# The last group of modulation columns, moved from the second down projection to the first

## The chip, the cores and the metric

The kernel runs on one core of one Trainium2 chip. The metric is device time in microseconds (us) of one execution, as the median of several runs. The engines are named as in the profile: PE (TensorE matmul) and PEld (its weight loads), DVE (VectorE), ACT (ScalarE), POOL (GpSimd) and SP (SyncE, whose queue issues all the loads and stores spoken of here). L12 is line 12 of the kernel before.

## What is computed

One layer of a streaming encoder on 512 tokens of 1024 channels, in float32: a SwiGLU feed-forward block, a token mixer (a gated delta rule beside latent attention) and a second feed-forward block. Each is scaled and shifted by columns that depend on the condition `c` alone:

```
mod = silu(c) @ w_ada + b_ada                                  # 9 x 1024 columns
sh1, s1, g1, sh2, s2, g2, sh3, s3, g3 = split(mod, 9)
h = rms(x) * (1 + s1) + sh1
x = x + 0.5 * g1 * ((silu(h @ w_gate) * (h @ w_up)) @ w_out)   # 1024 -> 2 x 2816 -> 1024
h = rms(x) * (1 + s2) + sh2
x = x + g2 * mixer(h)
h = rms(x) * (1 + s3) + sh3
x = x + 0.5 * g3 * ((silu(h @ w_gate2) * (h @ w_up2)) @ w_out2)
```

The change concerns the last 1024 of these columns, `g3`, which only the residual add of the second feed-forward block reads.

## The kernel before

**Layout and precision.** Channels lie on the 128 partitions, tokens along the free axis, so `x` is eight tiles of 128x512 (`self.xT`). A float32 product is made of three matmuls (`mm3`, L475 to L477): each operand is split into a high part and the rest, and high x high, high x low and low x high are summed in PSUM. A weight unit is 128 output columns by up to eight rows of 128: it is loaded to a raw tile `wr`, ACT casts the high part `wh` (L234) and DVE subtracts the low part `wl` (L235). Raw, high and low tiles have four buffers each.

**First down projection** (`down`, first call). Eight output tiles t = 0 to 7, each with three weight units of 8, 8 and 6 row blocks (`KPARTS`), so three parts of 24, 24 and 18 matmuls. After each part `down` gives side work a turn (`side.step`). A finished tile is added to `xT` by DVE (L1026), ACT squares it and DVE adds the square to `accum` for the next norm (L736 to L741). Tile 7 is made in two halves of 256 tokens in an order written out by hand (`in_order`), with the norm's sums over partitions (L761) and the first modulated tiles of the mixer between. The same function also makes the mixer's constants from tile 5 on: its first step (L1329 to L1341) issues small loads (to `cw`, `vb` and the positions), the second transposes `cw` on PE (L1345), the third transposes the positions (L1352).

**Modulation columns.** Group 0 (g1, sh2) is made in the first feed-forward block, groups 1 (s2, g2), 2 (sh3, s3) and 3 (g3) as side work by `ada_rest`. A group has four chunks of 512 columns, group 3 has two. For a chunk, eight row blocks of `w_ada` are loaded as 128x512 tiles (`ar`, SP) and summed on DVE with the entries of silu(c) as scalars (L826 for the first, L828 for the rest, into `aa`). One side step takes two row blocks: two loads and two sums. `ada_columns` then sums over partitions by a matmul with ones (L885), copies the rows (ACT, L888), transposes them back to columns (PE, L892), adds the bias (DVE, L896) and, for some columns, adds 1 or halves them (L901, L903). The loop of `ada_rest` runs these columns between the next group's sums; after the last group it adds two empty steps and then the columns.

**Second down projection** (`last_down`). `PLAN` lists its pieces: tiles 0 and 1 over all 22 row blocks ("all"), the tail (last six row blocks) of tiles 4 to 7, and then pairs of tiles by a form of seven products in place of eight (`seven_down`, L1244), for which `act_sums` makes sums of activations on DVE (L1127). Group 3 is made beside tile 1 and ended before the first tail (`side.flush`). Until then the accumulators of tiles 0, 1 and the first tail wait in `held`; the adds to `xT` (L1161), which need g3, follow together. A tile of the output is transposed on PE (L1294), copied by ACT and stored by SP (`store`); tiles 0 and 1 are stored inside the first pair by seven products.

**Order.** At the build, a scheduler makes one fixed queue per engine. It follows the order of the program among the instructions that are ready by its own estimate, so a weight split can come long before its place in the program, and PE work that is not ready goes behind later matmuls. Buffers are handed out in the same pass: 56 slots of 128x512 (`slots`) hold activations, `ar`, `aa` and most temporaries. At run time each engine works through its queue in order.

Of the kernel before, what the change touches and what calls it, by code (L numbers as in the profile page):

```python
# [99 lines left out]
class Block:  # L100
# [918 lines left out]
    def down(self, act, gate, norm=None):  # L1019

        nc = self.nc
        accum = self.slot(s="na") if norm else None
        full, ha, hb = slice(0, NT), slice(0, HALF), slice(HALF, NT)

        def update(t, ts, p):
            nc.vector.scalar_tensor_tensor(out=self.xT[t][:, ts], in0=p[:, ts], scalar=self.mod[gate][:, t:t + 1],  # L1026
                                           in1=self.xT[t][:, ts], op0=ALU.mult, op1=ALU.add)

        def finish(t, ts, p):
            update(t, ts, p)  # L1030
            if norm:
                self.square_in(t, ts, accum)

        def parts(t, ts, units=None, by=8, late=False):
            p = self.acc()
            for i, (k0, n) in enumerate(KPARTS):
                u = units[i] if units else self.next_unit()
                for k in range(0, n, by):
                    self.dense(p, u, act, ts, k, min(k + by, n), FT - 1, k0)
                    yield  # L1040
            if late:
                held.append((t, ts, p))
            elif norm and ts != full:
                update(t, ts, p)
            else:
                finish(t, ts, p)

        last = KT - 1
        side, held = Side(), []
        side.add(self.ada_rest((1, 2) if norm else (3,)))  # L1050
        if norm:
            self.consts = Side()
            self.consts.add(self.mixer_consts())

        def split_first():
            p = self.acc()
            for i, (k0, n) in enumerate(KPARTS):
                u = self.next_unit()
                for k in range(0, n, 2):
                    while any(not isinstance(a, tuple) for a in act[:k0 + k + 5]):  # L1060
                        self.splits.step()
                    self.dense(p, u, act, full, k, min(k + 2, n), FT - 1, k0)
                yield
            if norm:
                finish(0, full, p)
            else:
                held.append((0, full, p))

        for t in range(last):
            if norm and t == 1:  # L1070
                self.masks()
            for i, _ in enumerate(parts(t, full, late=not norm and t < 2) if t else split_first()):
                if t:
                    side.step(4 if not norm else 2)
                if norm and t == 5:
                    self.consts.step()
                if not norm and t > 2:
                    if i == 1:
                        self.store(t - 2, range(NB))
                elif not norm and t == 2:  # L1080
                    if i == 0:
                        side.flush()
                        for h in held:
                            finish(*h)
                    elif i == 1:
                        self.store(0, range(NB))
        units = [self.next_unit(ahead=0) for _ in KPARTS]
        if not norm:
            for i, _ in enumerate(parts(last, ha, units)):
                if i < 2:  # L1090
                    self.store(last - 2 + i, range(NB))
            for i, _ in enumerate(parts(last, hb, units)):
                if i == 1:
                    self.store(last, range(2))
            self.store(last, range(2, 4))
            return None
        with self.in_order():
            self.preload(3)
            for i, _ in enumerate(parts(last, ha, units)):
                if i == 0:  # L1100
                    side.step()
                if i == 1:
                    self.prefetch(1)
            side.flush()
            sa = self.square_half(last, ha)
            self.new_h()
            pa, pb = self.aux(), self.aux()
            na, nb = self.norm_half(0, pa, norm), self.norm_half(1, pb, norm)
            for i, _ in enumerate(parts(last, hb, units, 2)):
                if i == 0:  # L1110
                    self.add_sums(pa, accum[:, ha], first=True)
                    self.add_sums(pb, accum[:, hb], first=True)
                if i == 2:
                    self.add_sums(pa, sa, last=True)
                if i == 2 or i > 4:
                    next(na)
                if i == 4:
                    self.prefetch(2)
            self.prefetch(3)
            sb = self.square_half(last, hb)  # L1120
        return na, nb, lambda: self.add_sums(pb, sb, last=True)
# [30 lines left out]
    def last_down(self, act, gate):  # L1152

        nc = self.nc
        full = slice(0, NT)
        side, sums, parts7, ended, held = Side(), Side(), Side(), [], []
        side.add(self.ada_rest((3,)))
        sums.add(self.act_sums(self.whole))

        def update(t, ts, src):  # L1160
            nc.vector.scalar_tensor_tensor(out=self.xT[t][:, ts], in0=src, scalar=self.mod[gate][:, t:t + 1],  # L1161
                                           in1=self.xT[t][:, ts], op0=ALU.mult, op1=ALU.add)

        def ahead():
            self.preload(1)
            parts7.add(self.raws.pop(0)())

        def stores():
            while ended:
                self.store(ended.pop(0), range(NB))  # L1170
                yield

        for at, (kind, t) in enumerate(PLAN):
            after = [k for k, _ in PLAN[at + 1:at + 3]] + ["all"] * 2
            if kind in SEVENS:
                w, work = self.weights7, parts7
                if after[0] in SEVENS:
                    ahead()
                else:
                    work = Side()  # L1180
                    work.add(self.readied())
                self.seven_down(w, act, 8 * kind, t, update, work, stores())
                work.flush()
                if kind:
                    ended += [t, t + 1]
                elif after[0] not in SEVENS:
                    sums.add(self.act_sums(act[8:16]))
                continue
            p = self.acc()
            for i, (k0, n) in enumerate(KPARTS):  # L1190
                if i in MISSING[kind]:
                    continue
                u = self.next_unit(ahead=0 if i == 2 and after[0] in SEVENS else 1)
                if kind == "tail" and after[0] == "tail" and after[1] in SEVENS or (
                        i == (0 if kind == "most" else 1) and after[0] in SEVENS):
                    ahead()
                if at == 2:
                    side.flush()
                for k in range(0, n, 2):
                    while not at and any(not isinstance(a, tuple) for a in act[:k0 + k + 5]):  # L1200
                        self.splits.step()
                    for j in range(k, k + 2):
                        xh, xl = act[k0 + j]
                        self.mm3(p, u[0][:, j, :], u[1][:, j, :], xh, xl, k0 + j == (16 if kind == "tail" else 0),
                                 k0 + j == FT - 1)
                    if at == 1:
                        side.step()
                    if at > 1 or i == 2 and at:
                        sums.step()
                    parts7.step()  # L1210
                if ended and kind != "tail":
                    self.store(ended.pop(0), range(NB))
            held.append((t, p))
            if at > 1:
                for h, p in held:
                    update(h, full, p)
                    if kind == "all" or h < 2:
                        ended.append(h)
                held = []
            if after[0] in SEVENS:  # L1220
                sums.flush()
                parts7.flush()
# [1303 lines left out]
```

## Time and profile before

| | us |
|---|---|
| median of 3 runs | 1015.23 |
| fastest, slowest run | 1014.57, 1015.83 |
| the profiled execution, its own time | 1016.3 |
| span of the profile, first to last instruction | 1014.6 |

All times within the program are from the profiled execution. In a row of a timeline the first number is the start in us from the start of the span, the second the length; a bracket gives the idle time of the engine before it and what ended it. In a row of grouped instructions the numbers after the first bar are busy time in us and the mean of one in ns, after the second the idle time before them. In a row of waits they are the sum in us, the number of waits and the longest. SP rows show the issue of a load, not its transfer.

The first down projection runs from about 255 to 385 us, tiles 1 to 6 being some 15 to 16 us each, and the second from about 878 us to the end, its tile 1 from about 903 to 918 us.

### The profile page before, as it was taken

Reading aid. Unit: us, or ns where it says so; the run is one execution under the profiler, and the core shown is the slowest. Engines: PE = TensorE matmul, PEld = TensorE weight load, DVE = VectorE, ACT = ScalarE, POOL = GpSimd, SP = SyncE. Lnnn points to the kernel's source line nnn. Section 1 sums busy time; section 2 is a strip of 40 time slices with the busy share of each in tenths; the row PEclk is TensorE's granted clock in tenths of the full one; section 3 lists DMA queues with packets and bytes.
Section 4 is the critical chain, followed back from the end, with each engine's and each line's share of the span. In section 5 each row is a group of like instructions: output and inputs, shape, how many; then the busy total and the mean of one; then the engine's idle time right before and its main releaser. Section 6 shows DMA issues by size and latency. Waiting matters only on the chain.

```text
span 1014.6 us, 17859 instructions
## 1 busy us (share of the span) xinstructions
PE 1003.9 (99%) x7029; PEld 906.2 (89%) x7029; DVE 814.8 (80%) x1445; ACT 521.2 (51%) x942; POOL 30.6 (3%) x74
## 2 busy tenths in 40 slices
PE   7999999999999999999999999999999999999998
PEld 6788999999887899888888888999999999987988
DVE  4779999887797847778987649789888888788995
ACT  4454555556422225658756365375555555634443
POOL 0000000000200000100001012000000000000000
PEclk9999999999999999999999999999999999999999
DMA  9863564334588825321132021212333434372612
GB/s 319 295 202 101 170 205 144 107 108 117 172 306 286 299 65 165 102 61 44 48 77 69 24 63 43 83 49 83 99 111 98 116 93 121 107 259 65 177 42 63
DMA packets 204034, 130.84 MB, mean 129 GB/s; under 512 B 14497, under 2 KB 188590, under 8 KB 203950
## 3 DMA queue, kind: packets, MB, share of 16 engines
q1 hardware_dynamic: 203950, 129.70, 42.0%
q8 instruction: 55, 0.90, 0.3%
q14 instruction: 29, 0.24, 0.1%
HBM read 127.18 MB, written 2.49 MB: 128 GB/s over the span
## 4 chain that ended last, share of the span: by engine, by line
PE 92%; DVE 4%; DMA 1%; ACT 1%; SPq 1%; issue 1%; POOL 0%; DVEq 0%; ACTq 0%
PE pa L360 18%; PE pa L475 14%; PE pa L477 14%; PE pa L476 14%; PE pb L360 13%; PE pa L1244 3%; PE pb L1244 2%; DMA ar<-in_w_ada 1%; PE pb L2212 1%; SPq L139 1%; PE pb L475 1%; PE pb L476 1%; PE pb L477 1%; PE pb L2192 1%; PE pb L1749 1%; DVE cv L1693 1%
## 5 line engine op out<-in xcount | busy, mean ns | idle before, releaser
L275 DVE TENSOR_TENSOR wl<-wr,wh 128x1024 fp32r<-128x1024 f32 x114 | 138.6, 1220 | 34.7 <-ACT wh L279 34.4
L234 ACT CAST wh<-wr 128x1024 fp32r<-128x1024 f32 (+1 forms) x81 | 81.0, 1009 | 131.6 <-PE pa L476 118.2
L279 ACT CAST wh<-wr 128x1024 fp32r<-128x1024 f32 x114 | 116.6, 1051 | 22.4 <-DVE wr L275 19.9
L235 DVE TENSOR_TENSOR wl<-wr,wh 128x1024 fp32r<-128x1024 f32 (+1 forms) x81 | 94.1, 1167 | 37.4 <-ACT wh L234 36.1
L475 PE MATMUL pa<-hh,wh 128*128 128x512 f32 (+1 forms) x309 | 119.2, 386 | 0.0
L477 PE MATMUL pa<-hh,wl 128*128 128x512 f32 (+1 forms) x309 | 116.2, 376 | 0.0
L476 PE MATMUL pa<-hl,wh 128*128 128x512 f32 (+1 forms) x309 | 116.1, 376 | 0.0
L475 PE MATMUL pa<-ah,wh 128*128 128x512 f32 (+1 forms) x294 | 110.5, 376 | 0.0
L476 PE MATMUL pa<-al,wh 128*128 128x512 f32 (+1 forms) x294 | 110.0, 374 | 0.0
L477 PE MATMUL pa<-ah,wl 128*128 128x512 f32 (+1 forms) x294 | 109.7, 373 | 0.0
L275 DVE TENSOR_TENSOR wr<-wr,wr 128x512 f32<-128x512 f32 x114 | 78.4, 688 | 1.7
L828 DVE SCALAR_TENSOR_TENSOR aa<-ar,sc,aa 128x512 f32<-128x512 f32 x98 | 73.4, 749 | 7.7 <-DMA ar<-in_w_ada 6.0
L360 PE MATMUL pa<-th,wh 128*128 128x256 f32 x264 | 74.8, 283 | 0.2 <-ACT z L365 0.2
L360 PE MATMUL pa<-hh,wh 128*128 128x256 f32 x264 | 74.8, 283 | 0.0
L360 PE MATMUL pa<-hh,wl 128*128 128x256 f32 x264 | 74.7, 283 | 0.0
L360 PE MATMUL pa<-tl,wh 128*128 128x256 f32 x264 | 74.7, 283 | 0.0
L360 PE MATMUL pa<-th,wl 128*128 128x256 f32 x264 | 74.7, 283 | 0.0
L360 PE MATMUL pa<-hl,wh 128*128 128x256 f32 x264 | 74.7, 283 | 0.0
L475 PEld LDWEIGHTS pa<-hh,wh 128*128 128x128 f32 x309 | 58.4, 189 | 10.1 <-issue 1.6
L477 PEld LDWEIGHTS pa<-hh,wl 128*128 128x128 f32 x309 | 58.2, 188 | 10.1
L475 PEld LDWEIGHTS pa<-ah,wh 128*128 128x128 f32 x294 | 55.3, 188 | 12.2 <-ACT wh L234 2.5
L476 PEld LDWEIGHTS pa<-hl,wh 128*128 128x128 f32 x309 | 58.4, 189 | 8.5
(488 smaller groups left out, 2694.3 us busy)
## 6 DMA issues: line engine op xcount, KB each, us to landing
wr<-in_ffn_w_in SPq DMA_DIRECT2D x79, 512.0 KB
ar<-in_w_ada SPq DMA_DIRECT2D x128, 256.0 KB
wr<-in_ffn_w_out SPq DMA_DIRECT2D x32, 512.0 KB
wr<-in_w_in SPq DMA_DIRECT2D x21, 512.0 KB
wr<-in_ffn_w_out SPq DMA_DIRECT2D x16, 384.0 KB
wr<-in_w_out SPq DMA_DIRECT2D x8, 512.0 KB
wr<-in_ffn_w_in SPq DMA_DIRECT2D x8, 384.0 KB
ar<-in_w_ada SPq DMA_DIRECT2D x6, 512.0 KB
```

The lines of the kernel that those rows point to most:

```text
L139: return self.nc.sync.dma_start(dst, src)
L234: self.nc.scalar.copy(hi, raw)
L235: self.nc.vector.tensor_tensor(out=lo, in0=raw, in1=hi.bitcast(F32), op=ALU.subtract)
L275: sub = lambda out, x, y: nc.vector.tensor_tensor(out=out, in0=x, in1=y, op=ALU.subtract)
L279: nc.scalar.copy(hi[:, :n], raw[:, :n])
L360: nc.tensor.matmul(z, a[:, j, :], b, start=start and j == 0 and i == 0, stop=j == 3 and i == 2, skip_group_check=not start)
L475: mm(out, wh, xh, start=start, stop=False)
L476: mm(out, wh, xl, start=False, stop=False)
L477: mm(out, wl, xh, start=False, stop=stop)
L828: nc.vector.scalar_tensor_tensor(out=acc, in0=a, scalar=sc, in1=acc, op0=ALU.mult, op1=ALU.add)
L1244: nc.tensor.matmul(z, a[:, j, :], b, start=start and j == 0 and i == 0, stop=j == 3 and i == 2, skip_group_check=not start)
L1693: nc.vector.scalar_tensor_tensor(out=a[:, d:], in0=p[:, :NT - d], scalar=wj(3 - d), in1=a[:, d:], op0=ALU.mult, op1=ALU.add)
```

## The change

`down` gets all three groups: `ada_rest` is called with (1, 2, 3) there. The side work keeps two steps per part in tiles 1 to 3 and gets three in tiles 4 to 6. `last_down` loses group 3 with its flush and the `held` list: each tile is added to `xT` at its own end, tiles 0 and 1 are free for the store from there, and the act sums get a turn in the whole of tile 1 where they had one in its last part. Branches of `down` for a call without a norm, which is not made in this kernel, change with it. The loads, sums and columns of the group are the same.

```diff
@@ down
-        side.add(self.ada_rest((1, 2) if norm else (3,)))
+        side.add(self.ada_rest((1, 2, 3)))
...
                 if t:
-                    side.step(4 if not norm else 2)
+                    side.step(2 if t < 4 else 3)
@@ last_down
-        side, sums, parts7, ended, held = Side(), Side(), Side(), [], []
-        side.add(self.ada_rest((3,)))
+        sums, parts7, ended = Side(), Side(), []
         sums.add(self.act_sums(self.whole))
...
-                if at == 2:
-                    side.flush()
...
-                    if at == 1:
-                        side.step()
-                    if at > 1 or i == 2 and at:
+                    if at:
                         sums.step()
                     parts7.step()
...
-            held.append((t, p))
-            if at > 1:
-                for h, p in held:
-                    update(h, full, p)
-                    if kind == "all" or h < 2:
-                        ended.append(h)
-                held = []
+            update(t, full, p)
+            if kind == "all":
+                ended.append(t)
```

## The prediction

> **What bounds the kernel now.** I read the page's busy times first, then TensorE's waits, longest first, then busy times by stretch, and last the timelines of the queues around the two places of the change.
>
> ```profile
> span 1014.6 us, 17859 instructions
> PE 1003.9 (99%) x7029; PEld 906.2 (89%) x7029; DVE 814.8 (80%) x1445; ACT 521.2 (51%) x942; POOL 30.6 (3%) x74
> PE pb L526 <- DMA xt<-in_x: 4.6, 1, 4.6
> PE pb L2212 <- ACT pT L2208: 0.5, 1, 0.5
> ...
> PE pa L360 <- ACT z L365: 0.2, 1, 0.2
> ```
>
> TensorE (PE) is busy for all but 10.7 us of the span. Its longest wait, 4.6 us, is at the very start for the input; every other one is 0.5 us or less. Here are the stretches that matter, with columns window, its length, busy time and count of PE, PEld, DVE, ACT, POOL, then the granted clock, the DMA share and GB/s:
>
> ```profile
> 267.00:272.00 5.00, 5.00 (x24) 4.14 (x23) 1.99 (x4) 1.72 (x3) 0.00 (x0) 1.00 0.46 144
> 277.00:282.00 5.00, 5.00 (x24) 4.14 (x23) 4.57 (x6) 0.61 (x2) 0.00 (x0) 1.00 0.97 344
> 286.00:301.40 15.40, 15.40 (x70) 12.75 (x69) 13.58 (x19) 3.93 (x5) 0.00 (x0) 1.00 0.98 326
> 316.60:332.50 15.90, 15.90 (x77) 12.24 (x76) 11.30 (x18) 3.42 (x6) 0.00 (x0) 1.00 0.88 297
> 332.50:348.00 15.50, 15.50 (x69) 12.31 (x68) 12.09 (x19) 3.62 (x5) 1.12 (x32) 1.00 0.81 261
> 316.60:363.20 46.60, 46.60 (x213) 36.88 (x215) 35.16 (x53) 10.48 (x14) 1.12 (x32) 1.00 0.80 261
> 363.20:400.00 36.80, 36.80 (x308) 35.82 (x305) 20.65 (x44) 13.59 (x25) 1.82 (x3) 1.00 0.37 105
> 900.00:923.00 23.00, 23.00 (x103) 17.83 (x102) 18.77 (x32) 5.36 (x8) 0.00 (x0) 1.00 0.81 269
> 923.00:940.00 17.00, 17.00 (x91) 14.62 (x89) 16.59 (x30) 8.83 (x13) 0.00 (x0) 1.00 0.09 23
> ```
>
> The first three rows lie in tiles 0 to 2 of the first down projection. Rows four and five are its tiles 4 and 5, row six its tiles 4 to 6 together, where the change adds work; 900 to 923 us is where it takes work away. PE is busy for the whole of each. So in both places VectorE (DVE) and the DMAs work beside a PE that never waits, and only what makes PE wait, or takes a wait from it, can move the end.
>
> **The change part by part.** Group 3 is two column chunks of eight rows each: 16 loads, 16 VectorE sums, then two matmuls by ones (L885), a ScalarE copy (L888), four transposes (L892) and two small VectorE operations.
>
> ```profile
> ar<-in_w_ada SPq DMA_DIRECT2D x128, 256.0 KB
> L828 DVE SCALAR_TENSOR_TENSOR aa<-ar,sc,aa 128x512 f32<-128x512 f32 x14 | 10.5, 749 | 0.4 <-DMA ar<-in_w_ada 0.2
> L826 DVE TENSOR_SCALAR aa<-ar,sc 128x512 f32<-128x512 f32 x2 | 1.0, 482 | 0.0
> 918.39 0.39 PE L477 MATMUL pa<-ah,wl 128*128 128x512 f32 x1
> 918.71 1.05 PE L885 MATMUL pb<-aa,ones 128*32 128x512 f32 x4
> 919.70 0.50 PE L475 MATMUL pa<-ah,wh 128*128 128x512 f32 x1
> 920.03 0.39 PE L476 MATMUL pa<-al,wh 128*128 128x512 f32 x1
> 920.26 0.39 PE L477 MATMUL pa<-ah,wl 128*128 128x512 f32 x1
> 920.49 0.40 PE L475 MATMUL pa<-ah,wh 128*128 128x512 f32 x1
> 920.82 0.46 PE L892 MATMUL pb<-ident,rw 64*128 64x64 f32 x4
> 921.21 0.50 PE L476 MATMUL pa<-al,wh 128*128 128x512 f32 x1
> 921.54 0.39 PE L477 MATMUL pa<-ah,wl 128*128 128x512 f32 x1
> ```
>
> *Taken from the second down projection.* Successive 512-column matmuls start 0.23 us apart (920.03, 920.26, 920.49). Against that pace the two insertions take (919.70 - 918.39 - 0.23) + (920.03 - 919.70 - 0.23) + (921.21 - 920.49 - 0.23) + (921.54 - 921.21 - 0.23) = 1.08 + 0.10 + 0.49 + 0.10 = 1.77 us of PE there. The change carries the same instructions to the first down projection: minus 1.77, plus 1.77, net 0. VectorE is rid of 10.5 + 1.0 = 11.5 us and the DMAs of 16 x 0.262 = 4.19 MB, beside a PE that is 23.00 of 23.00 us busy: 0. The residual adds of tiles 0 and 1 no longer wait for the group, the stores of these tiles and the act sums start earlier; they are the same instructions, and PE is full from 923 to 940 us too: 0.
>
> *Added to the first down projection.* A group step is two loads and two sums. Tiles 1 to 3 keep two steps per part (18 steps), tiles 4 to 6 get three (27): 45, and the three groups need 16 + 16 + 8 steps of sums, two empty ones and three for the last columns, also 45. So the group ends with tile 6, its L885 where group 2's stands now. Steps 19 to 40, 44 sums instead of 28, fall in tiles 4 to 6: VectorE goes from 35.16 to 35.16 + 11.5 = 46.7 us in 46.60, its whole time. DMA goes from 261 x 46.6 = 12.2 MB to 16.4 MB. At the 326 GB/s of the row with a 0.98 share that takes 50.2 us, 3.6 too many; at the 344 of the five microseconds before, 47.6 us, 1.0 too many. Both run late, then; I take the 3.6, from the longer stretch. What covers that?
>
> ```profile
> 344.03 0.96 DVE L235 TENSOR_TENSOR wl<-wr,wh 128x768 fp32r<-128x768 f32 x1 [2.20 <-ACT wh L234]
> 355.70 3.90 DVE L828 SCALAR_TENSOR_TENSOR aa<-ar,sc,aa 128x512 f32<-128x512 f32 x5
> 359.78 0.96 DVE L235 TENSOR_TENSOR wl<-wr,wh 128x768 fp32r<-128x768 f32 x1 [0.18 <-ACT wh L234]
> 363.18 0.75 DVE L1026 SCALAR_TENSOR_TENSOR xT<-pa,mod,xT 128x512 f32<-128x512 f32 x1 [2.44 <-PE pa L477]
> 362.75 0.39 PE L477 MATMUL pa<-ah,wl 128*128 128x512 f32 x1
> 363.07 1.06 PE L885 MATMUL pb<-aa,ones 128*32 128x512 f32 x8
> 373.23 0.95 PE L761 MATMUL pb<-ones,na 128*128 128x1 f32 x8
> ```
>
> There is one 128x768 split per tile; that of 344.03 is tile 6's third unit, that of 359.78 tile 7's. Tile 6's last matmul starts at 362.75, and the unit has 18 of them, so it starts near 362.75 - 17 x 0.23 = 358.8, against a split done at 344.03 + 0.96 = 345.0: 13.8 us ahead. That is the cover of the weights that stand behind the sums in VectorE's queue, more than the 3.6 us. The norm's sums need tile 6's add only at 373.23, 10 us after 363.18. On SP, weight loads are held by the release of raw tiles, and they fall behind six loads per part instead of four; their splits have the same 13.8 us. POOL has only the constants' 32 small operations (1.12 us), wanted in the mixer.
>
> Here a rule of the Trainium skill speaks against the change: HBM Reference, section Specifications (TRN2), gives a core about 358 GB/s, though its note lets a core that streams alone reach more. By that figure the 16.4 MB would take an estimated 45.8 of the 46.6 us: no room to catch up, but no lateness either, where the 326 GB/s row gives 3.6 us of it. The trace here neither reaches the figure over a whole tile nor shows what limits the 326.
>
> Two PE instructions have less cover. L885 starts 363.07; the sums before it end at 355.70 + 3.90 = 359.6, a margin of 3.5 us. The new last sums end about 3.6 us later, so the margin is used up: a wait of 0.1 us, between 0 (if the queue order of the build puts L885 later among tile 7's matmuls) and 3.7 (if the loads lag twice as far). The other is the constants' transpose:
>
> ```profile
> 339.98 0.22 SPq L139 DMA_DIRECT2D cw<-in_mla_out_norm_w  x1
> 345.50 0.14 PEld L1345 LDWEIGHTS pb<-ident,cw 57*128 57x128 f32 x1 [0.35 <-DMA ar<-in_w_ada]
> ```
>
> L1345's weight load already sits idle for 0.35 us until a DMA (the row names an ar load; its own operand is cw, from the small loads). By then four or five parts have issued two more loads each ahead of these: 8 x 0.262 = 2.1 MB, 6.4 us at 326 GB/s, of which the idle shares of tile 4 (0.12 x 15.9 = 1.9 us) and a third of tile 5 (0.19 x 5.2 = 1.0 us) take 2.9. That is up to 3.5 us later at L1345, and PE's queue stands behind it. Lower end 0, where the build moves the transpose back as it does today (it stands 5.5 us after the last of these loads). I take 0.3, near today's 0.35, since every wait of PE in this trace is 0.5 us or less.
>
> Sum against the profiled execution: 1014.6 + 0 (moved PE work) + 0 (VectorE, DMA) + 0.3 = 1014.9 us of span, and its own time goes from 1016.3 to 1016.6. That execution stands 1.1 us above the median of the runs, 1015.23; the same sum on the median gives 1015.5. A gain below nothing is bounded by what PE loses between its start and its last microseconds: 0.94 in the mixer stretch and 0.46 and 0.35 in two others.
>
> ```profile
> 165.00:180.00 15.00, 14.54 (x119) 14.14 (x118) 13.48 (x21) 6.66 (x14) 0.00 (x0) 1.00 0.52 161
> 400.00:610.00 210.00, 209.06 (x1568) 175.80 (x1567) 157.92 (x385) 131.87 (x266) 13.30 (x14) 1.00 0.24 65
> 610.00:680.00 70.00, 69.65 (x521) 66.20 (x520) 57.19 (x130) 36.27 (x83) 5.84 (x7) 1.00 0.17 52
> ```
>
> **The rivals.** Slower: the lateness reaches PE's queue, in tile 5 at L1345 or after tile 6 at L885. It decides from the point where SP's small loads land more than 2.0 us later than the build's order allows for. Price: the 3.5 us worked out above at one of the two, since a wait at L1345 gives the loads time before L885: 1015.2 + 3.5 = 1018.7. For it speak a VectorE at 46.7 of 46.60 us and DMAs at 351 GB/s of demand; against it, that the order already allows for waits of this kind almost to the half microsecond.
>
> Faster: PE is busy but not at its peak, and gives time back when VectorE is relieved at 900 to 923 us. Weight loads fill 17.83 of 23.00 us, 78%, so the array might have room. Perfetto Trace Analysis of the Trainium skill, section Identifying the Most-Contended Engine, says just that matmul busy time misjudges headroom and weight-load time should be read instead. The trace agrees that the two shares differ, and no more. Against the rival: from 267 to 272 us VectorE is busy 1.99 of 5.00 us, from 277 to 282 us 4.57, and PE does 24 matmuls with 4.14 us of weight loads in both. A pace better by 0.01 us, the last digit of a start, would be 1.0 us over the 23.00 / 0.23 = 100 matmuls: 1014.2, still no measurable gain.
>
> The change does not do what it says: a step short, and columns are left for tile 7's flush. Then PE takes the same 1.77 us there; 1015.2 to 1015.5. And the moved buffers re-deal the build's order elsewhere: at best the 1.75 us of the three rows above, 1013.5; at worst as much lost.
>
> **How the numbers follow.** A measurement of this kernel tells about 0.2%, 2.0 us, from no change. Forecast, with the step-short case: 0.70, at 1015.5. Lateness that reaches PE by more than 2 us: 0.22, at 1018.7. VectorE's relief: 0.03, at 1014.2, in the same band. Re-dealt order: 0.05, of which 0.02 faster by over 2 us, and 0.02 slower by as much, if more is gained or lost than the waits show. Same 0.70 + 0.03 + 0.01 = 0.74; slower 0.22 + 0.02 = 0.24; faster 0.02. The range runs from 1014.0, the relief and a little of the re-deal, to 1018.7, the slower rival's price.
>
> **What would show it.** Right: no wait of PE over 0.5 us from 316 to 400 us; VectorE at 45 us or more of the 46.6 in tiles 4 to 6; the group's L885 near 363 us and none near 918; tile 1 of the second down projection with 11.5 us less on VectorE and PE still full. Wrong: idle of PE or PEld before L1345 or L885 that is put down to a DMA or to VectorE; weight splits less than 2 us ahead of their matmuls in tile 7; or PE's start-to-start pace other than 0.23 us in either place.

## The result, and the profile after

The changed kernel took 1023.38 us (median of 5 runs, 1021.52 to 1024.53) against 1015.45 us before (5 runs, 1014.57 to 1015.95): a ratio of 1.0074, with a 95% interval of 1.0060 to 1.0088. It is 7.9 us slower, where 1015.5 us, no change, was forecast, and it lies beyond the forecast's upper end of 1018.7. The profiled execution took 1024.06 us, its span is 1022.3 us. Line numbers are those of each kernel; in the changed one those below `down` are lower by 1 to 9 (L1345 is now L1336, L1347 is L1338).

The page's busy times and TensorE's waits of the changed kernel, as before the sum, the number and the longest in us:

```profile
span 1022.3 us, 17873 instructions
PE 1008.1 (99%) x7029; PEld 908.5 (89%) x7029; DVE 815.1 (80%) x1445; ACT 521.1 (51%) x942; POOL 30.6 (3%) x74
PE pb L526 <- DMA xt<-in_x: 4.7, 1, 4.7
PE pb L885 <- DVE aa L828: 1.3, 1, 1.3
PE pb L761 <- DVE mod L903: 0.9, 1, 0.9
PE pb L1834 <- DVE t L1472: 0.7, 1, 0.7
PE pb L892 <- ACT rw L888: 0.7, 1, 0.7
```

PE's busy time grew by 4.2 us (1003.9 to 1008.1) for the same 7029 matmuls, and three of the four new waits hang on the moved columns: L885, L892, and the norm's sums L761 behind `mod`. Busy times by stretch of the changed kernel, in the columns used before (length, PE, PEld, DVE, ACT, POOL, granted clock, DMA share, GB/s):

```profile
316.60:333.10 16.50, 16.50 (x79) 12.76 (x78) 11.30 (x17) 4.02 (x6) 0.00 (x0) 1.00 0.90 306
333.10:348.00 14.90, 14.90 (x67) 12.33 (x67) 14.07 (x20) 3.42 (x5) 0.00 (x0) 1.00 0.78 266
348.00:366.40 18.40, 18.40 (x82) 13.17 (x81) 12.56 (x24) 4.02 (x6) 1.12 (x32) 1.00 1.06 360
366.40:376.00 9.60, 9.60 (x75) 8.63 (x73) 8.09 (x13) 0.98 (x1) 0.00 (x0) 1.00 0.51 154
376.00:381.70 5.70, 2.72 (x18) 1.50 (x16) 2.32 (x6) 1.42 (x3) 0.00 (x0) 1.00 0.00 0
382.40:385.70 3.30, 3.30 (x17) 3.30 (x17) 0.16 (x1) 0.00 (x0) 0.70 (x1) 0.50 0.02 5
```

The first three rows are tiles 4 to 6, the fourth is tile 7's first half and the first six matmuls (two row blocks) of its second half. Up to 376.00 us PE waits for nothing. Then come 5.7 us in which it works 2.72, and after them 3.3 us at a granted clock of 0.50. Here is PE's timeline around these places (start, length; a bracket gives the idle time before and what ended it; in L885 a chunk counts as x2):

```profile
352.70 1.06 PE L885 MATMUL pb<-aa,ones 128*32 128x512 f32 x6
357.78 1.05 PE L885 MATMUL pb<-aa,ones 128*32 128x512 f32 x2
369.51 1.04 PE L885 MATMUL pb<-aa,ones 128*32 128x512 f32 x2
375.98 0.28 PE L477 MATMUL pa<-ah,wl 128*128 128x256 f32 x1
377.57 1.05 PE L885 MATMUL pb<-aa,ones 128*32 128x512 f32 x2 [1.31 <-DVE aa L828]
379.34 0.46 PE L892 MATMUL pb<-ident,rw 64*128 64x64 f32 x4 [0.72 <-ACT rw L888]
380.75 1.02 PE L761 MATMUL pb<-ones,na 128*128 128x1 f32 x8 [0.95 <-DVE mod L903]
381.63 0.36 PE L475 MATMUL pa<-ah,wh 128*128 128x256 f32 x1
382.97 0.41 PE L477 MATMUL pa<-ah,wl 128*128 128x256 f32 x1
383.18 0.41 PE L475 MATMUL pa<-ah,wh 128*128 128x256 f32 x1
```

Three things are to be seen. **Split columns:** group 2's four chunks went as three and one (352.70, 357.78), group 3's two as one and one (369.51, 377.57), and an L885 event takes 1.05 us with one chunk as with three. Before, group 2's four stood in one event at 363.07. **A wait in the open:** after 375.98, the sixth of the 66 matmuls of tile 7's second half, PE's queue has only the columns' chain and L761 ahead of the other 60 (the expectations below call this place "between the halves"; the first half's last matmul starts at 375.26). **A low clock:** at 383 us the 256-column matmuls start 0.21 us apart (382.97, 383.18), where those of tile 7's first half start 0.12 us apart.

VectorE's timeline tells why the columns were late:

```profile
352.80 0.22 DVE L1338 COPY cwT<-pb 128x57 f32<-128x57 f32 x1 [2.17 <-PE pb L1336]
361.80 0.19 DVE L896 TENSOR_TENSOR mod<-pb,vT 128x16 f32<-128x16 f32 x1 [2.97 <-PE pb L892]
371.07 3.10 DVE L828 SCALAR_TENSOR_TENSOR aa<-ar,sc,aa 128x512 f32<-128x512 f32 x4
375.58 0.48 DVE L1026 SCALAR_TENSOR_TENSOR xT<-pa,mod,xT 128x256 f32<-128x256 f32 x1 [1.41 <-PE pa L477]
375.98 1.53 DVE L828 SCALAR_TENSOR_TENSOR aa<-ar,sc,aa 128x512 f32<-128x512 f32 x2
379.84 0.17 DVE L896 TENSOR_TENSOR mod<-pb,vT 128x8 f32<-128x8 f32 x1 [2.32 <-PE pb L892]
379.92 0.68 DVE L741 TENSOR_TENSOR na<-na,sq 128x512 f32<-128x512 f32 x1
```

It stood 2.17 us before the constants' copy and 2.97 us before group 2's columns (0.82 and 1.59 before the change), with sums queued behind both; then it worked almost without a gap, 11.59 us of the 11.73 from 362.44 to 374.17. There it stood again, for 1.41 us: group 3's last two sums are behind the add of tile 7's first half (375.58) in its queue, and that add needs the half's last matmul. Their loads were not what they waited for: the last was issued by 364.94 us, and from 371 to 372 us the DMA share was 0.00. Ahead of the add they would have ended near 374.17 + 1.53 = 375.7 us, an estimate, and PE's work lasts to 375.98 + 0.28 = 376.26. So this wait of 1.31 us goes back to a place in VectorE's queue, which the build had fixed. Behind group 3's own L896 then stands the last square of the norm (L741, 379.92), which L761 needs.

SP's issues, first two rows of the kernel before, then of the changed one:

```profile
340.25 2.72 SPq L139 DMA_DIRECT2D ar<-in_w_ada  x6
345.44 3.96 SPq L139 DMA_DIRECT2D ar<-in_w_ada  x6
```

```profile
349.87 6.77 SPq L139 DMA_DIRECT2D ar<-in_w_ada  x8
358.60 6.34 SPq L139 DMA_DIRECT2D ar<-in_w_ada  x6
```

The last load of a row block is issued by 364.94 us in place of 349.40, 15.5 us later.

**Where the 7.9 us are.** After its start the kernel repeats itself from one execution to the next so closely that the same matmul, counted along PE's queue, can be laid side by side in two traces. Its later start against the kernel before is the lag. It grows by 2.2 us up to the end of tile 7's first half: two more L885 events, about 1.1 us each with the edges. At L761 (380.75 against 373.23 before) it has grown by 4.65 us more: 1.31 + 0.72 + 0.95 = 2.98 us of waits, and 1.67 us of L885 and L892 themselves. The low clock adds 1.6. That is 8.5 us in the first down projection; the mixer adds 0.6 (about the new wait of 0.7 at L1834), and the second down projection gives 1.8 back by 990 us: 7.3. Another 0.2 comes back behind that, in every kernel without the group there. With the lag of 0.65 at the start this makes 7.7, the difference of the two spans (1022.3 and 1014.6).

### The profile page after: what moved, and what is told of

It is laid out like the page before. It is cut to its first block, busy times and chain, and to the rows that moved or that the text cites. A ratio compares the mean times of both kernels' runs of the same rounds, so it can differ in the third digit from the quotient of the medians.

```text
span 1022.3 us, 17873 instructions
## 1 busy us (share of the span) xinstructions
PE 1008.1 (99%) x7029; PEld 908.5 (89%) x7029; DVE 815.1 (80%) x1445; ACT 521.1 (51%) x942; POOL 30.6 (3%) x74
## 4 chain that ended last, share of the span: by engine, by line
PE 89%; DVE 6%; DMA 2%; issue 1%; ACT 1%; SPq 0%; POOL 0%; DVEq 0%; ACTq 0%
PE pa L360 17%; PE pa L475 14%; PE pa L477 14%; PE pa L476 14%; PE pb L360 12%; PE pa L1235 3%; PE pb L1235 2%; DMA ar<-in_w_ada 1%; PE pb L2183 1%; PE pb L475 1%; PE pb L477 1%; PE pb L476 1%; DVE cv L1684 1%; PE pb L2203 1%; PE pb L1740 1%
## 5 line engine op out<-in xcount | busy, mean ns | idle before, releaser
L477 PEld LDWEIGHTS pa<-ah,wl 128*128 128x128 f32 x294 | 55.9, 190 | 11.4 <-issue 1.7
```

Source lines behind the costliest of these rows:

```text
L477: mm(out, wl, xh, start=False, stop=stop)
```

## The experiments

The table gives, for every kernel that was run, the lag behind the kernel before at 280 us (one execution's start), what it grew by in the first down projection, the mixer and the second down projection (to 990 us), the sum of these three, and the timed median less that of the kernel before in the same session. The lags are worked out from the traces, one execution each; all in us.

| kernel | start | first down | mixer | second down | sum of the three | timed |
|---|---|---|---|---|---|---|
| changed | 0.65 | 8.49 | 0.62 | -1.80 | 7.3 | 7.9 |
| old_tail | -0.21 | 9.58 | 0.05 | -1.82 | 7.8 | 7.9 |
| cols_joined | -2.08 | 9.00 | 0.00 | -1.81 | 7.2 | 6.4 |
| no_sum3 | -1.33 | 7.26 | 0.02 | -1.82 | 5.5 | 5.0 |
| consts_early | -1.24 | 4.18 | 0.21 | -1.81 | 2.6 | 2.5 |
| no_load3 | -0.83 | 3.96 | 0.16 | -1.80 | 2.3 | 1.4 |
| cols_late | -1.94 | 1.02 | 2.65 | -1.81 | 1.9 | 1.2 |
| pace3_joined | -0.93 | 3.19 | 0.10 | -1.80 | 1.5 | 1.6 |
| late_joined | -0.57 | 0.57 | 2.63 | -1.79 | 1.4 | 1.2 |
| before_short | -1.72 | 0.78 | 0.07 | 0.00 | 0.9 | 0.9 |
| before_again | -1.06 | 0.02 | -0.04 | 0.00 | 0.0 | -0.1 |
| no_group3 | 2.27 | 0.03 | 0.05 | -1.77 | -1.7 | 0.4 |
| no_second | 2.05 | 0.02 | 0.22 | -1.85 | -1.6 | 0.9 |

The sum of the three agrees with the timed difference to 0.9 us in every kernel but the last two, of which more below.

**cols_late: the columns alone.** Group 3's loads and sums as in the changed kernel, its columns handed to the side work of the mixer.

```diff
+        if hold:
+            self.held_columns = waiting
+            return
...
-        side.add(self.ada_rest((1, 2, 3)))
+        side.add(self.ada_rest((1, 2, 3), True))
...
+        self.consts.add(self.held_columns)
```

> Group 3's loads and sums stay in the first down projection as in the changed kernel; only its columns (L885, L888, L892, L896) move out of tile 7, into the mixer's first dense units beside the constants. Theory A (the loss is the wait of TensorE for these columns between the halves of tile 7, 376 to 382 us, with the half clock behind it): the wait of 3.4 us and the 1.6 us of half clock go, and the two column matmuls run side by side in one place, 1.0 us less: 1023.4 - 6 = about 1017.4. Theory B (the 16 more loads and sums crowd the weights' path in tiles 4 to 6, wherever the columns stand): 1022 to 1023.

Measured: 1017.43 us (10 runs), ratio 1.0016 (1.0006 to 1.0026), the granted clock 1.00 throughout tile 7. All 16 loads and 16 sums in the first down projection cost 1.0 us there, which is one more event of group 2's columns. The other 7.5 us of the changed kernel's 8.5 come with group 3's columns in their place; about 1.7 of them are the columns themselves, while the mixer, which has them instead, loses 2.65 us, 2.0 more than the changed kernel's.

**no_load3 and no_sum3: what makes the columns late.** In the first the sums of group 3 read a tile that is there already, in the second the loads stay and 14 of 16 sums are cut to 8 columns.

```diff
+        if g == 3:
+            return [self.xT[KT - 1]] * 2
```

> Group 3's 16 loads are left out; its sums read a tile of x instead, so g3 is not the reference's. VectorE has the same 16 sums. Theory A1 (the columns are late because their loads are late): the sums end some 5 us earlier, the columns fall inside the first half of tile 7 and TensorE waits under 0.5 us: 1017 to 1019. Theory A2 (they are late because VectorE is full): 1022 to 1023, with the wait of TensorE at 376 to 382 us still there.

```diff
+                    if c > 11 and kc + e:
+                        nc.vector.scalar_tensor_tensor(out=acc[:, :8], in0=a[:, :8], scalar=sc, in1=acc[:, :8], op0=ALU.mult,
+                                                       op1=ALU.add)
```

> All 16 loads of group 3 stay; 14 of its 16 sums take 8 columns instead of 512, so g3 is not the reference's. Theory A1 (late loads): columns still after the first half of tile 7, wait still 2 to 3 us, 1021 to 1023. Theory A2 (VectorE full): sums end earlier by about 14 x 0.6 = 8 us, no wait, 1017 to 1018.

Measured: 1017.65 us (8 runs), ratio 1.0020 (1.0010 to 1.0030), without the loads; 1021.17 us (2 runs only), ratio 1.0055 (1.0034 to 1.0075), with short sums. Without the loads the same number of sums end in time, the last of them ahead of the add of tile 7's first half; PE has no wait in tile 7, there is no low clock, and the 4.0 us left are those of three L885 events and an L892. With short sums the waits of L892 and L761 (0.72 and 0.95 us) and the low clock stay, the wait for L885 is 0.26 us. Here are the busy times of two stretches of no_sum3, then VectorE's timeline (a short sum has L826 there, the add of the half L1029):

```profile
348.00:366.40 18.40, 18.40 (x83) 12.64 (x81) 10.62 (x25) 4.05 (x5) 1.12 (x32) 1.00 1.01 349
380.00:383.25 3.25, 3.25 (x17) 3.25 (x17) 0.16 (x1) 0.76 (x1) 0.70 (x1) 0.50 0.02 5
```

```profile
367.10 1.27 DVE L826 SCALAR_TENSOR_TENSOR aa<-ar,sc,aa 128x8 f32<-128x8 f32 x5
373.67 0.48 DVE L1029 SCALAR_TENSOR_TENSOR xT<-pa,mod,xT 128x256 f32<-128x256 f32 x1 [5.29 <-PE pa L477]
374.07 0.48 DVE L826 SCALAR_TENSOR_TENSOR aa<-ar,sc,aa 128x8 f32<-128x8 f32 x2
```

DMA is nearly as full as in the changed kernel while VectorE has 7.8 of 18.4 us free, and PE still falls to 0.50: the last sums do not want for VectorE's time. Nor do they wait for their loads here, though both times are those expected of late loads: the last was issued by 359.98 us, and the DMAs moved 3 GB/s from 366 to 367 us, but VectorE stood idle for 5.29 us with the last two sums behind the add, as in the changed kernel. In no_load3, and below in consts_early and pace3_joined, these sums stand ahead of the add, and PE does not wait. The build orders what is ready by its own estimate; loads that are late in that estimate would put the sums behind the add, and sums without loads are ready early. That fits these traces, but no kernel was run with only the two sums moved ahead of the add, so it is not shown.

**consts_early: the constants out of the way.** The constants get their first step in tile 2; nothing else in the program is changed.

```diff
-                if norm and t == 5:
+                if norm and t == 2:
```

> As the changed kernel, but the mixer's constants get their first step (the small loads) in tile 2 of the first down projection in place of tile 5. Loads, sums and steps of the three groups are unchanged; the constants' transpose, behind which VectorE's queue stood in tile 6, is long past, and the build's order puts group 3's columns and L892 some 18 matmuls ahead of the end of tile 7's first half. The split column events stay (5, as in the changed kernel). Theory A (three costs: split events, the chain waited for between the halves, the low clock after it): the last two go, 1018.3 (1017.3 to 1019.3), with the clock at 1.00 throughout tile 7. Theory B (any columns within tile 7 cost as much as those of the changed kernel): 1022 or more.

Measured: 1018.05 us (9 runs), ratio 1.0029 (1.0019 to 1.0038): 5.3 us of the 7.9 are gone. PE's timeline:

```profile
364.76 1.05 PE L885 MATMUL pb<-aa,ones 128*32 128x512 f32 x2
371.68 1.04 PE L885 MATMUL pb<-aa,ones 128*32 128x512 f32 x2
373.57 0.46 PE L892 MATMUL pb<-ident,rw 64*128 64x64 f32 x4
376.21 0.95 PE L761 MATMUL pb<-ones,na 128*128 128x1 f32 x8
```

The same columns still stand in tile 7, one chunk at a time, but ahead of the end of its first half, and L885, L892 and L761 have no wait. The clock stays at 1.00 from 374 to 390 us. The first down projection still costs 4.18 us: three events of about 1.15 with their edges, and 0.6 for L892. This run shows that the place of the constants' first step, with its eight small loads and the copy that waits for them, was enough to push the chain past the end of the half. It does not tell the queues' blocking at run time from the build's order, for that changed with it: the last six sums run from 366.90 us, ahead of the add of the half (375.69).

**before_short: the place alone, with early sums.** The kernel before, one step a part in tile 6, so that group 2's columns fall in tile 7.

```diff
-                    side.step(4 if not norm else 2)
+                    side.step(2 if t < 6 else 1)
```

> The kernel before, with one step of the side work a part in tile 6 in place of two, and nothing added: group 2's columns and its L892 come late and stand within tile 7, between its halves or close to it. Theory A (TensorE's wait comes from the chain last sum, columns, row, L892, L896 and the square add of tile 6 queued behind it, wherever the columns stand so, but with their sum early only the part from the columns on is waited for): 1017 to 1021. Theory B (the position costs nothing, only late loads do): 1015.0 to 1016.2.

Measured: 1016.41 us (10 runs), ratio 1.0009 (0.9999 to 1.0018), between the two expectations. In PE's timeline L892 stands right behind L885:

```profile
369.27 1.06 PE L885 MATMUL pb<-aa,ones 128*32 128x512 f32 x8
371.09 0.66 PE L892 MATMUL pb<-ident,rw 128*128 128x128 f32 x4 [0.76 <-ACT rw L888]
372.30 0.95 PE L761 MATMUL pb<-ones,na 128*128 128x1 f32 x8
```

The place costs one wait of 0.76 us for the copy of the rows between them (0.78 in the table). Columns in tile 7 whose sums are done are cheap; late sums make them dear.

**cols_joined and late_joined: the split.** The matmuls of a group are ordered behind that group's last sum.

```diff
+            if after:
+                self.follow(mm.ins, after)
```

> As the changed kernel, but the chunks' column matmuls of L885 of a group all wait for that group's last sum, so that each group's chunks stand side by side on TensorE: one event a group (before the changed kernel's 5 events in the first down projection: 1+2+2; here 3). Group 3's columns and its L892 stay between the halves of tile 7. Theory A (the split events cost about 1 us of TensorE each, whatever number of chunks is in one): 2 events fewer, 1021.4 (1020.7 to 1022.2); the wait between the halves and the low clock after it stay. Theory B (an event costs by its chunks, so that a split costs nothing): 1023.4, as the changed kernel. Theory C (the wait between the halves is all that costs): 1023.0 to 1023.8.

> As cols_late (group 3's loads and sums as in the changed kernel, its columns in the mixer), with the column matmuls of each group held together as in cols_joined. Theory A (a split costs about 1 us an event): two events fewer than cols_late, so 1017.4 - 2 = 1015.4 (1015.0 to 1016.4), no measurable difference from the kernel before. Theory B (a split costs nothing, cols_joined's 1.5 us is from the shorter wait): 1017.0 to 1018.0.

Measured: cols_joined 1021.88 us (4 runs), ratio 1.0062 (1.0047 to 1.0077); late_joined 1016.73 us (11 runs), ratio 1.0011 (1.0002 to 1.0020). The first number is as expected, but its trace doesn't bear the reason out. Here are PE's columns in cols_joined and its stretch of low clock:

```profile
371.86 1.05 PE L886 MATMUL pb<-aa,ones 128*32 128x512 f32 x2
374.02 1.04 PE L886 MATMUL pb<-aa,ones 128*32 128x512 f32 x2 [1.12 <-DVE aa L828]
```

```profile
377.50:384.25 6.75, 6.75 (x33) 6.75 (x33) 0.16 (x1) 0.77 (x1) 0.70 (x1) 0.50 0.01 2
```

The chunks are next to each other in the queue and yet not in time: the first ran and PE waited for the second one's sum. Group 2's joined event took 1.60 us in place of two of 1.05. And in this execution the low clock lasted 6.75 us, so that the first down projection lost 9.0 us, not less than the changed kernel. late_joined gained 0.4 us in the first down projection on cols_late, not 2: cols_late had one split to be joined, not two as I had counted, and the joined event again took 1.6 us. The time of late_joined lies between its two expectations. What a split costs is read from consts_early, then, not from these two.

**pace3_joined: everything ahead of tile 7.** As cols_joined, three steps a part from tile 1 on.

```diff
-                    side.step(2 if t < 4 else 3)
+                    side.step(3)
```

> As cols_joined, but with three steps of the side work in each part of the down projection from tile 1 on in place of two up to tile 3: the three groups' loads, sums and columns come earlier, and group 3's columns and L892 stand ahead of tile 7. All of the added work stays in the first down projection. Theory A (the loss is where the columns stand: the wait of TensorE between the halves of tile 7, the low clock after it, and the split events): 1015.0 to 1017.0, since none of the three is left. Theory B (the added 16 loads and sums in the first down projection cost by themselves, by DMA traffic or VectorE time): 1019 or more.

Measured: 1017.07 us (10 runs), ratio 1.0015 (1.0006 to 1.0025), just over the upper end of the first theory's range; no wait of the columns and a clock of 1.00. All the moved work is in the first down projection, and 6.3 us of the 7.9 are gone. What is left in the trace is 3.2 us there, against 1.8 given back: group 3's event and L892, about 2.2, and 1 us more since group 1's event waits for a sum in its middle (2 us long in place of 1.05).

**old_tail, no_second, no_group3 and before_again: the second down projection.** old_tail has the changed first down projection and puts back only the old order of the second one, without the group. no_second is the kernel before with group 3 left out there. no_group3 is the changed kernel without group 3 anywhere. before_again is the kernel before, unchanged.

```diff
-        side.add(self.ada_rest((3,)))
...
+        self.mod[8] = self.mod[5]
```

These lines are no_second's; no_group3 has `ada_rest((1, 2))`, two steps a part and the same second line.

> The changed first down projection, and in the second one the order of the kernel before (updates of tiles held back, the act sums' order) without the group's steps: only the second down projection's rewritten order is undone. Theory A (all of the loss stems from the first down projection and the second one gains the removed group's time in either order): 1022.9 to 1024.0, as the changed kernel. Theory B (the new order of the second down projection costs or gains by itself): more than 0.8 us off 1023.4.

> The kernel before with group 3 left out of the second down projection and not made anywhere (g3 is taken from another group's columns): the half of the change that takes away, alone; the first down projection and the order of the second one's updates are those of the kernel before. Theory A (the removed columns' 1.77 us of TensorE come back in full): 1.8 us under the kernel before, 1013.7 (1013.2 to 1014.3). Theory B (what is taken away there is lost again, or in the spread of the start): within 0.6 us of the kernel before.

> Group 3 is left out altogether (the last residual add takes g2 in place of g3); first down projection as before, second as changed. Theory A: the first down projection is that of before, the second loses 1.77 us of TensorE work: 1015.4 - 1.8 = 1013.6. If the second down projection's earlier adds, stores and act sums cost by themselves (rival C): 1014.5 or more.

> The kernel before once more, as a kernel of its own, nothing changed. It tells how far two builds of one program lie apart in the timed runs, since every variant so far lies 0.4 to 1.6 us over the kernel before, also where its trace shows no such loss. Theory A (the timing is blind to which of the two it is): within 0.3 us. Theory B (a kernel that is not the shared kernel before starts later): 0.5 to 1.2 us slower.

Measured: old_tail 1023.39 us (4 runs), ratio 1.0075 (1.0060 to 1.0090), as the changed kernel, and the second down projection gives the same 1.8 us back: its new order neither costs nor gains. The 1.1 us more that its profiled execution lost in the first down projection came at the low clock, which lasted twice as long there (6.8 us). before_again 1015.47 us (11 runs), ratio 0.9999 (0.9991 to 1.0008): a program timed under another name is timed alike, and after its start its trace stays within 0.05 us of the kernel before.

no_second took 1016.49 us (11 runs), ratio 1.0007 (0.9998 to 1.0016), and no_group3 1016.60 us (10 runs), ratio 1.0009 (0.9999 to 1.0018). Both were expected some 2 us under the kernel before, and both missed; no_second lies over its second expectation too, and no_group3's time, in the band of its rival, says nothing for that rival since the table shows no such cost. The table shows the second down projection faster by 1.85 and 1.77 us, as in every kernel without the group there; it is the start that is later. In the start their PE and SP queues have the order of the kernel before. Here are two stretches of no_second, then of before_again:

```profile
10.00:15.00 5.00, 4.08 (x35) 2.77 (x34) 1.58 (x9) 2.72 (x8) 1.03 (x1) 1.00 1.18 307
15.00:20.00 5.00, 5.00 (x38) 3.44 (x37) 3.42 (x8) 1.52 (x3) 0.00 (x0) 1.00 1.18 308
```

```profile
10.00:15.00 5.00, 4.66 (x38) 3.31 (x37) 2.17 (x9) 3.17 (x7) 0.91 (x1) 1.00 1.13 356
15.00:20.00 5.00, 5.00 (x35) 3.39 (x34) 3.09 (x6) 1.16 (x3) 0.00 (x0) 1.00 1.11 361
```

The DMAs are as busy, and move 307 GB/s where they move 356 in before_again; no_group3 shows 308 and 307. The kernel before, whose own start is 1.06 us later than that of before_again, shows 336 and 332. By 280 us PE is 3.1 us (no_second) and 3.3 us (no_group3) behind before_again; that the slower loads are the reason is likely, but not shown. The other runs of these two builds lie about as high as their profiled one, so it may belong to the build; each start was seen in one trace alone. Why these two read more slowly stays open.

## Why the prediction was wrong

**Right.** PE took the same work in the second down projection as 1.77 us, and its removal gives 1.77 to 1.85 by 990 us in every trace without it. VectorE's 11.5 us and the 4.19 MB that went there with it are worth next to nothing, as said (the 0.2 us that come back later are all that is left for them); the new order of adds, stores and act sums neither (old_tail). VectorE's relief and the re-dealt order, the two faster cases, didn't show. The direction of the slower rival was right: the loads and sums ran late, up to L885.

**Wrong: "So the group ends with tile 6, its L885 where group 2's stands now", and "The new last sums end about 3.6 us later".** This is the step that failed. The step count says where the steps stand in the program, not when they run. Group 2's last loads were issued by 349.40 us, 13 us ahead of tile 6's last matmul at 362.75; the sums had that lead to run late in. From 316.60 to 363.20 us SP's queue had this to wait for (the longest rows before, then after):

```profile
SPq L139 <- DVE wl L235: 29.3, 9, 8.1
SPq L139 <- DMA ar<-in_w_ada: 2.2, 6, 0.5
```

```profile
SPq L139 <- DVE wl L235: 5.1, 3, 3.4
SPq L139 <- DMA ar<-in_w_ada: 4.6, 14, 0.8
SPq L139 <- DMA wr<-in_ffn_w_out: 3.9, 3, 1.5
```

Before, it waited 29.3 us for weight buffers: it was ahead of its work. The added loads used that lead up (5.1 us left), and part of the wait passed to the row blocks. I set a rate against a demand over the whole stretch and called the difference, 3.6 us, the lateness. The last loads came 15.5 us later and the last sum ended at 377.5 us, where group 2's had ended at 359.6: 17.9 us. Part of it was in my own count: step 40 of 45 lies in tile 6's second part, where group 2's last sums lay in its first, a part being 24 x 0.23 = 5.5 us. Another part is the place of the last two sums behind the add of tile 7's first half: all sums ahead of it had ended at 374.17, 3.3 us earlier. How the rest divides between SP's used-up lead and VectorE's stops stays open.

**Wrong: VectorE "46.7 us in 46.60, its whole time".** It was busy 11.30 + 14.07 + 12.56 = 37.9 us in the 49.8 of tiles 4 to 6. In these tiles it was not full but blocked, 2.17 and 2.97 us before a copy and an add that needed PE; the sums so put off filled it in tile 7 (11.59 of 11.73 us). The prediction looked for L1345's cost in PE's queue (0.3 us) and found none to speak of; PE had none. The copy behind it held up VectorE, with the sums in its queue; taking it and its small loads away from there gave 5.3 us (consts_early, which changes the build's order with them).

**Wrong: "columns are left for tile 7's flush. Then PE takes the same 1.77 us there".** I took the place to be free. Tile 7's order is written out by hand, with the norm's sums after the second half's first six matmuls, and nothing stands there to fill in for a late chain of sum, L885, copy, L892, L896 and the square queued behind it: 2.98 us of waits. The slower rival had the mechanism, a late L885, but its price of 3.5 us, worked out for late small loads at L1345, comes near the 2.98 us of these waits by luck. It left out the splits (2.2 us), which come since PE takes each chunk when its sum is done, and the clock that falls after a stretch with little work (1.6 us).

**The DMA rate.** The rate of 326 GB/s that I took from one stretch is no bound: the changed kernel moved 360 GB/s over 18.4 us. That agrees with the Trainium skill's HBM Reference, section Specifications (TRN2), by which a core has about 358 GB/s and one that streams alone may have more. The last loads came 15.5 us later all the same.

**What would have shown it** were the signs named: waits over 0.5 us from 316 to 400 us (three: L885, L761, L892), no L885 near 363. VectorE at 45 us or more, named as a sign of being right, did not come either (37.9 in 49.8). The pace was 0.23 us up to tile 7, as said.

## What to carry to other kernels

Before side work is added, read how far ahead of need its queue runs (here SP's 29.3 us of waits for buffers, and loads issued 13 us early): here added loads used that lead up first, and the rate against the demand did not show it. Then ask what stands ahead of the late instruction and behind it on every engine's queue, and whether the place where it lands has other work for TensorE; a short chain in a hand-ordered stretch can cost its whole length, as here. None of the versions tried beats the kernel before: the 1.8 us that a group's columns take from PE in the second projection come back as at least as much in the first or in the mixer, and only splits and waits differ.

## What the runs showed of the hardware

**Side-by-side chunks.** L885's chunks lie on different 32-column groups of the array, and one, three or four of them take 1.04 to 1.06 us together. The Trainium skill, TensorE: Matmul & The Clock Gate, Part 3: Packing small matmuls, says that such tiles run at the same time; the rows agree. What follows is that splitting such a group costs a full event each time.

**The clock.** It fell to 0.50 after 5.7 us with 2.72 us of work in them, though no single wait of PE was over 1.31 us. By the traces' clock records it stayed there for 3.4 us in the changed kernel and in no_sum3, where PE was busy for the whole of the 3.3 us shown, and for 6.8 us in cols_joined and in old_tail. The same page of the Trainium skill, in the sections What's actually happening and HAM oscillation, has windows of about 3.4 us, after an idle one of which the rate is halved: lengths of one and two windows agree with that, but its rule of thumb of no idle gap over some 3 us does not warn of this case, where the gaps are short and the work between them is little. Every kernel with this chain of waits in tile 7 showed the fall in the first down projection (changed, old_tail, cols_joined, no_sum3) and none of the others did; the fall by itself, without the waits, was not tried.

**The start.** Two executions of the kernel before differed by 1.06 us: 0.8 in the first 30 us, the rest up to 204 us, and from there on they repeated each other to 0.05 us. Two builds with the same order on PE and SP there read at 307 to 308 GB/s from 10 to 20 us, in place of 356 to 361 in before_again, and were 3.1 and 3.3 us behind it. So here a change of 0.2% is better read from lags behind the start than from the times.
